# Attention scores with a full-row low part of the key, and RWKV output sums collected by kind of product

## The chip, the cores and the metric

The kernel runs on one core of one Trainium2 chip. The metric is the device time of one execution in microseconds (us); where several runs are given, it is their median. Engines go by the names of the profile: PE is TensorE (PEld its weight loads), DVE is VectorE, ACT is ScalarE, POOL is GpSimd, SP is SyncE.

## What is computed

One sequence of 512 tokens with 1024 channels passes a first block of two hybrid layers (eight attention heads of 64 channels and four retention heads of 128), a feed-forward layer, a token mixer (pooling, a gated linear attention called hgrn, RWKV-7 and a second gated linear attention called gla), a second feed-forward layer. The two places that the change touches are these, cut from the reference:

```python
# chunked_rel_attention
scores = jnp.where(valid, scores + bias[None, None], NEG_INF)
p = jax.nn.softmax(scores, axis=-1)
out = jnp.einsum("bnhqk,bnkhd->bnqhd", p, vb)

# rwkv7_scan, per head with S in (N_v, N_k)
s_kk = jnp.einsum('bhvk,bhk->bhv', S, kk_t)
S = (S * w_t[:, :, None, :] - s_kk[..., None] * (kk_t * a_t)[:, :, None, :]
     + v_t[..., :, None] * k_t[:, :, None, :])
return S, jnp.einsum('bhvk,bhk->bhv', S, r_t)
```

`scores` is the product of queries and keys of one head. The RWKV output is then normalised over each head's 64 channels.

## The kernel before

All products are of fp32 quality. The large ones split each operand into a high and a low part (type fp32r) and take three matmuls: high·high, low·high and high·low. These are the lines L210 to L212, called `mm`, 128x512 each, which make up most of PE's work. The smaller ones, transposes among them, are fp32 matmuls, for which the trace has two records each.

**First block.** `layer` runs eight units p. For p < 4 a unit projects the queries, keys, values and gate of two attention heads; for p >= 4 of one retention head. The scores, the softmax and the product with the values of unit p - 1 (`core()`) are emitted behind the projections of unit p, so that PE finds projection matmuls (`mm`) to run while the softmax goes on; the scheduler sets the final order of each engine's queue. A tile of 128 rows holds both heads' q and k, 64 channels (rows) each. `stacked` (L415 to L431) splits them for the scores. In `qs` of head h the rows of the head (`own`) hold the high part of q and the other 64 rows its low part; `ks` holds the high part of k in both halves. So one matmul over 128 rows, L456, gives high·high plus low·high. The third product needs the low part of k, `kl`: one tile for both heads, each head in its own 64 rows, made by a DVE subtraction for each head (L429, 64x512). L457 multiplies with it over 64 rows: PE then works as an array of 64 rows and 128 columns, which the trace writes as 64*128, and not as 128*128.

`attention` goes over four blocks t of 128 queries; block t needs 128(t + 1) keys. For both heads it takes the scores into a PSUM bank of the pool `psa` (two banks), adds the bias and takes the maximum on DVE (L463, one instruction with a second one that reads the accumulator), the exponential on ACT (L466), the reciprocal and the scaling on DVE (L467, L468). PE transposes the result (`pt`, L472), ACT copies it (`pT`, L474), and PE multiplies it with the values (`po`, L480, an array of 128*64). In the same stretch DVE scales projection results (L395: `fa` is q, `k`, `g` the gate) and splits weights (L189), and ACT casts weights (L188).

**Retention** (p >= 4) loads a tile `decay` by a DMA on SP's queue (two buffers).

**Mixer.** The four mixers are generators, whose steps are run in an order written out by hand (`MIX_ORDER`). RWKV is worked in two halves c of two heads each, with eight chunks n of 64 tokens. Its last step sums the output `pO` (L1072 to L1087), for each chunk n and head h: RH·S (the state, none for n = 0; L1082, array 128*64), MN·KV (L1084, 64*64) and LQ·X (L1086, 64*64). Chunk n lies in the 64-row half n % 2 of one PSUM bank, and the three matmuls of each (n, h) are one accumulation group. 46 matmuls, 92 records; the whole stands twice in the program, for c = 0 and c = 1. Then DVE takes statistics (L1091 to L1097), ACT normalises (`on`, L1100), DVE scales and adds (L1102, L1104), PE transposes (`pt`, L1107).

Of the kernel before, what the change touches and what calls it, by code (L numbers as in the profile page):

```python
# [8 lines left out]
F32 = mybir.dt.float32  # L9
F32R = mybir.dt.float32r  # L10
# [3 lines left out]
ALU = mybir.AluOpType  # L14
# [3 lines left out]
T = 512  # L18
D = 1024
NT = T // 128  # L20
# [92 lines left out]
class Build:  # L113
# [235 lines left out]
    def layer(self, l):  # L349
        nc = self.nc  # L350
        b1 = self.b1
# [60 lines left out]
                nc.scalar.activation(out=t[:, tt, :], in_=ps, func=AF.Copy, scale=rtm[:, tt:tt + 1])  # L412
            return t

        def stacked(q, k):  # L415


            qs, ks = [], []
            kl = b1.tile([128, T], F32R, tag="kl", name="kl", bufs=2)
            for h in range(2):  # L420
                own, other = slice(64 * h, 64 * h + 64), slice(64 - 64 * h, 128 - 64 * h)
                t = b1.tile([128, T], F32R, tag="qs", name="qs", bufs=4)
                nc.scalar.copy(t[own], q[own])
                nc.vector.tensor_tensor(out=t[other], in0=q[own], in1=t[own].bitcast(F32), op=ALU.subtract)
                qs.append(t)
                t = b1.tile([128, T], F32R, tag="ks", name="ks", bufs=4)
                nc.scalar.copy(t[own], k[own])
                nc.scalar.copy(t[other], k[own])
                nc.vector.tensor_tensor(out=kl[own], in0=k[own], in1=t[own].bitcast(F32), op=ALU.subtract)  # L429
                ks.append(t)  # L430
            return qs, (ks, kl)  # L431

        def gate(g, u):
            t = scaled(g, u, 0.5, "g", 8)
# [5 lines left out]
        def attention(p, q, k, v, g):  # L440

            po = self.psc.tile([128, T], F32, tag="c", name="po")
            bias = []
            for h in range(2):
                t = b1.tile([128, T], F32, tag="bias", name="bias", bufs=4)
# [3 lines left out]
            for t in range(NT):  # L449
                n = 128 * (t + 1)  # L450
                pss = []
                for h in range(2):
                    hr = slice(64 * h, 64 * h + 64)
                    ps = self.psa.tile([128, T], F32, tag="a", name="s")[:, :n]
                    qt = q[h][:, t * 128:(t + 1) * 128]
                    nc.tensor.matmul(ps, lhsT=qt, rhs=k[0][h][:, :n], start=True, stop=False)  # L456
                    nc.tensor.matmul(ps, lhsT=qt[hr], rhs=k[1][hr, :n], start=False, stop=True)  # L457
                    pss.append(ps)
                pts = []
                for h in range(2):  # L460
# [9 lines left out]
                    for kt in range(t + 1):  # L470
                        ks = slice(kt * 128, (kt + 1) * 128)
# [44 lines left out]
        v = None  # L516
        for p in range(8):
            if p < 4:
                q = scaled(0, p, 0.125, "fa", 2, self.tmp)
                k = scaled(1, p, 1.0, "k", 2)  # L520
                q, k = stacked(q, k)
            else:
                if p == 4:
                    nc.gpsimd.tensor_tensor(out=CR, in0=self.cosT, in1=R, op=ALU.mult)
                    nc.gpsimd.tensor_tensor(out=SR, in0=self.sinT, in1=R, op=ALU.mult)
                q = rotated(4, p - 4, "qs")
                k = rotated(5, p - 4, "ks")
            if p % 2 == 0:
                v = values(vw if p == 0 else vload(2 if p < 4 else 6, (p % 4) // 2))
            g = gate(3 if p < 4 else 7, p % 4)  # L530
            y.append(g)
            if core is not None:
                core()
            if l == 0 and p == 1:
                self.tables()
            core = (lambda f=(attention if p < 4 else retention), a=(p % 4, q, k, v, g): f(*a))
# [300 lines left out]
    def rwkv(self, e, c):  # L837
# [9 lines left out]
        def psa(shape, name):  # L847
            return self.psa.tile([128, *shape], F32, tag="a", name=name)
# [219 lines left out]
        for tp in range(2):  # L1068
            nc.vector.tensor_tensor(out=bv[:, 4 * tp:4 * tp + 4, :].rearrange("p (i h) k -> p i h k", h=2),
                                    in0=KV[tp][:, :, 128:256].rearrange("p i (h k) -> p i h k", h=2),  # L1070
                                    in1=sb[:, 8 + 4 * tp:12 + 4 * tp].rearrange("p (i h) -> p i h", h=2).unsqueeze(3).to_broadcast([128, 2, 2, 64]), op=mult)
        po = psa((8, 64), "pO")  # L1072
        for tt in range(NT):
            tp, i = tt // 2, tt % 2
            for cc in range(2):
                r = slice(64 * cc, 64 * cc + 64)
                n = 2 * tt + cc
                for h in range(2):
                    v = 2 * i + h
                    pv = po[r, 2 * tt + h, :]  # L1080
                    if n:
                        nc.tensor.matmul(pv, lhsT=RH[:, h, 64 * n:64 * n + 64], rhs=S[:, n, :],  # L1082
                                         start=True, stop=False)
                    nc.tensor.matmul(pv, lhsT=MN[tp][r, v, 64:128],  # L1084
                                     rhs=KV[tp][r, i, 128 + 64 * h:192 + 64 * h], start=(n == 0), stop=False)
                    nc.tensor.matmul(pv, lhsT=LQ[r, 2 * tt + h, 64:128], rhs=X[tp][r, v, 64:128],  # L1086
                                     start=False, stop=True)  # L1087
        st = self.sm.tile([128, 8, 6], F32, tag="bst", name="bst", bufs=2)
        mv = self.sm.tile([128, 8, 2], F32, tag="bmv", name="bmv", bufs=2)
        for j in range(8):  # L1090
# [395 lines left out]
```

## Time and profile before

| | us |
|---|---|
| median of 3 runs (1694.39 to 1697.08) | 1695.64 |
| the profiled execution | 1697.89 |
| its span in the trace | 1696.1 |
| PE busy | 1669.0 (98%) |
| DVE busy | 986.6 (58%) |
| ACT busy | 628.9 (37%) |

The profiled execution stands 2.25 us above the median, within 1 us of the slowest of the three runs. Its mean granted TensorE clock is 0.988 of full speed. A row of the timeline gives an instruction's start and its recorded duration; PE's matmuls are pipelined, so what one of them costs the queue is the distance from its start to the next start, not the recorded duration.

### The profile page before, as it was taken

To read this page: it belongs to the slowest core of one execution; us is meant where nothing else is said; L and a number is where in the kernel's file an instruction comes from. 1 tells how busy PE (TensorE), PEld (TensorE's weight loads), DVE (VectorE), ACT (ScalarE), POOL (GpSimd) and SP (SyncE) were. 2 spreads that over 40 slices of the span, in tenths; PEclk is the share of its full clock that TensorE was granted. 3 is DMA by queue.
4 is the path that set the end of the run, shared out by engine and by line. 5 is a ranking of instruction groups with operands and counts; after the bars stand their busy time and mean duration, and the time that the engine had idled before them with its cause. 6 is when DMAs were issued, how large, how long until landed. Compare 5 with 4: busy or idle time off the path is not lost.

```text
span 1696.1 us, 24094 instructions
## 1 busy us (share of the span) xinstructions
PE 1669.0 (98%) x9648; PEld 1337.3 (79%) x9648; DVE 986.6 (58%) x1972; ACT 628.9 (37%) x1077; POOL 62.8 (4%) x59
## 2 busy tenths in 40 slices
PE   8999999999999999999999999999989999999998
PEld 6777787777778788888888877777767888888886
DVE  7684756554475765555533477658858655554322
ACT  6553423454342433222322235327434423332222
POOL 0001110000111000000000100000200000000000
PEclk9999999999999999999999999989979999999999
DMA  8221213422121223333333432212112433333331
GB/s 242 83 84 41 82 56 99 138 75 75 50 81 56 75 86 101 99 100 94 90 113 111 128 87 66 55 38 54 30 38 86 127 97 91 99 99 94 96 98 62
DMA packets 270673, 147.33 MB, mean 87 GB/s; under 512 B 10576, under 2 KB 264288, under 8 KB 270560
## 3 DMA queue, kind: packets, MB, share of 16 engines
q1 hardware_dynamic: 265600, 140.40, 28.6%
q0 software_dynamic: 1280, 4.20, 0.8%
q10 hardware_dynamic: 3680, 1.19, 0.3%
q8 instruction: 76, 1.25, 0.3%
q14 instruction: 37, 0.30, 0.1%
HBM read 141.30 MB, written 4.46 MB: 86 GB/s over the span
## 4 chain that ended last, share of the span: by engine, by line
PE 90%; DVE 6%; ACT 2%; DMA 1%; issue 1%; SPq 0%; DVEq 0%; ACTq 0%; POOLq 0%
PE mm L211 25%; PE mm L212 25%; PE mm L210 25%; PE po L480 2%; PE pt L472 1%; PE s L457 1%; PE po L498 1%; PE s L493 1%; PE s L456 1%; DMA wraw<-in_w_in 1%; DVE wlo L189 1%; PE pO L1084 1%; PE pO L1082 1%; DVE xr L1187 0%; PE bc L286 0%
## 5 line engine op out<-in xcount | busy, mean ns | idle before, releaser
L188 ACT CAST whi<-wraw 128x1024 fp32r<-128x1024 f32 (+2 forms) x244 | 245.1, 1005 | 691.5 <-PE mm L211 479.9
L189 DVE TENSOR_TENSOR wlo<-wraw,whi 128x1024 fp32r<-128x1024 f32 (+2 forms) x244 | 286.9, 1178 | 150.2 <-ACT whi L188 149.5
L593 DVE SCALAR_TENSOR_TENSOR fa<-mm,R 128x512 f32<-128x512 f32 x44 | 30.3, 691 | 107.8 <-PE mm L212 107.8
L589 DVE SCALAR_TENSOR_TENSOR fa<-mm,R 128x512 f32<-128x512 f32 x44 | 30.3, 690 | 90.5 <-PE mm L212 89.2
L210 PE MATMUL mm<-z0h,whi 128*128 128x512 f32 x163 | 67.7, 416 | 5.7 <-ACT z0h L203 5.7
L211 PE MATMUL mm<-z0l,whi 128*128 128x512 f32 x163 | 65.7, 403 | 0.0
L211 PE MATMUL mm<-z7l,whi 128*128 128x512 f32 x163 | 64.8, 398 | 0.9 <-DVE z7l L204 0.9
L212 PE MATMUL mm<-z0h,wlo 128*128 128x512 f32 x163 | 65.6, 402 | 0.0
L210 PE MATMUL mm<-z4h,whi 128*128 128x512 f32 x163 | 65.4, 401 | 0.0
L210 PE MATMUL mm<-z5h,whi 128*128 128x512 f32 x163 | 65.3, 401 | 0.0
L210 PE MATMUL mm<-z7h,whi 128*128 128x512 f32 x163 | 64.5, 395 | 0.7 <-ACT z7h L203 0.7
L212 PE MATMUL mm<-z3h,wlo 128*128 128x512 f32 x163 | 65.1, 399 | 0.0
L210 PE MATMUL mm<-z6h,whi 128*128 128x512 f32 x163 | 65.1, 399 | 0.0
L212 PE MATMUL mm<-z4h,wlo 128*128 128x512 f32 x163 | 65.0, 399 | 0.0
L211 PE MATMUL mm<-z4l,whi 128*128 128x512 f32 x163 | 65.0, 399 | 0.0
L211 PE MATMUL mm<-z3l,whi 128*128 128x512 f32 x163 | 65.0, 399 | 0.0
L212 PE MATMUL mm<-z6h,wlo 128*128 128x512 f32 x163 | 64.9, 398 | 0.0
L211 PE MATMUL mm<-z5l,whi 128*128 128x512 f32 x163 | 64.6, 396 | 0.0
L211 PE MATMUL mm<-z6l,whi 128*128 128x512 f32 x163 | 64.6, 396 | 0.0
L212 PE MATMUL mm<-z1h,wlo 128*128 128x512 f32 x163 | 64.5, 396 | 0.0
L211 PE MATMUL mm<-z2l,whi 128*128 128x512 f32 x163 | 64.5, 396 | 0.1
L210 PE MATMUL mm<-z2h,whi 128*128 128x512 f32 x163 | 64.5, 395 | 0.0
(738 smaller groups left out, 4230.6 us busy)
## 6 DMA issues: line engine op xcount, KB each, us to landing
wraw<-in_w_in SPq DMA_DIRECT2D x90, 512.0 KB, 4.1
wraw<-in_ffn_w_in SPq DMA_DIRECT2D x88, 512.0 KB, 3.8
wraw<-in_ffn_w_out SPq DMA_DIRECT2D x32, 512.0 KB, 3.9
wraw<-in_w_out SPq DMA_DIRECT2D x16, 512.0 KB, 4.3
wraw<-in_ffn_w_out SPq DMA_DIRECT2D x16, 384.0 KB, 3.6
bias<-in_relb SPq DMA_DIRECT2D x16, 256.0 KB, 2.9
x<-in_xT SPq DMA_DIRECT2D x8, 256.0 KB, 5.3
decay<-in_decay SPq DMA_DIRECT2D x8, 256.0 KB, 3.1
```

The lines of the kernel that those rows point to most:

```text
L188: nc.scalar.copy(hi[:, ks, :], raw[:, ks, :])
L189: nc.vector.tensor_tensor(out=lo[:, ks, :], in0=raw[:, ks, :], in1=hi[:, ks, :].bitcast(F32), op=ALU.subtract)
L210: mm(out, lhsT=lh, rhs=rh, start=start, stop=False)
L211: mm(out, lhsT=lh, rhs=rl, start=False, stop=False)
L212: mm(out, lhsT=ll, rhs=rh, start=False, stop=stop)
L456: nc.tensor.matmul(ps, lhsT=qt, rhs=k[0][h][:, :n], start=True, stop=False)
L457: nc.tensor.matmul(ps, lhsT=qt[hr], rhs=k[1][hr, :n], start=False, stop=True)
L472: nc.tensor.transpose(pt[:, ks], s[:, ks], self.ident)
L480: nc.tensor.matmul(po[64 * h:64 * h + 64, t * 128:(t + 1) * 128], lhsT=v[:, kt, vc:vc + 64], rhs=pts[h][:, ks], start=(kt == 0), stop=(kt ...
L493: nc.tensor.matmul(ps, lhsT=k[:, kt * 128:(kt + 1) * 128], rhs=q[:, T - n:], start=True, stop=True)
L589: nc.vector.scalar_tensor_tensor(out=a2, in0=pg, scalar=0.5, in1=R, op0=ALU.mult, op1=ALU.mult)
L593: nc.vector.scalar_tensor_tensor(out=a2, in0=pu, scalar=0.5, in1=R, op0=ALU.mult, op1=ALU.mult)
```

## The change

Two parts, which have nothing to do with each other.

**Scores.** `stacked` makes one `kl` tile for each head and writes the low part of k into both halves, by two subtractions instead of one: 16 subtractions of 64x512 before, 32 after. The tiles of unit p take the buffers of `decay` for even p and those of `kl` for odd p. The second score matmul (L458 after, L457 before) then uses all 128 rows, as the first does, and so also adds low·low.

**RWKV output.** The 46 matmuls are the same, but go in three parts: all of RH·S, then all of MN·KV, then all of LQ·X, each with n falling from 7 to 0. One accumulation group for each 64-row half of the bank takes the place of one for each (n, h).

```diff
--- before.py
+++ after.py
@@ -412,11 +412,10 @@
                 nc.scalar.activation(out=t[:, tt, :], in_=ps, func=AF.Copy, scale=rtm[:, tt:tt + 1])
             return t
 
-        def stacked(q, k):
-
-
-            qs, ks = [], []
-            kl = b1.tile([128, T], F32R, tag="kl", name="kl", bufs=2)
+        def stacked(q, k, spare):
+
+
+            qs, ks, kls = [], [], []
             for h in range(2):
                 own, other = slice(64 * h, 64 * h + 64), slice(64 - 64 * h, 128 - 64 * h)
                 t = b1.tile([128, T], F32R, tag="qs", name="qs", bufs=4)
@@ -426,9 +425,12 @@
                 t = b1.tile([128, T], F32R, tag="ks", name="ks", bufs=4)
                 nc.scalar.copy(t[own], k[own])
                 nc.scalar.copy(t[other], k[own])
-                nc.vector.tensor_tensor(out=kl[own], in0=k[own], in1=t[own].bitcast(F32), op=ALU.subtract)
                 ks.append(t)
-            return qs, (ks, kl)
+                kl = b1.tile([128, T], F32R, tag=spare, name="kl", bufs=2)
+                for half in (own, other):
+                    nc.vector.tensor_tensor(out=kl[half], in0=k[own], in1=t[own].bitcast(F32), op=ALU.subtract)
+                kls.append(kl)
+            return qs, (ks, kls)
 
         def gate(g, u):
             t = scaled(g, u, 0.5, "g", 8)
@@ -450,11 +452,10 @@
                 n = 128 * (t + 1)
                 pss = []
                 for h in range(2):
-                    hr = slice(64 * h, 64 * h + 64)
                     ps = self.psa.tile([128, T], F32, tag="a", name="s")[:, :n]
                     qt = q[h][:, t * 128:(t + 1) * 128]
                     nc.tensor.matmul(ps, lhsT=qt, rhs=k[0][h][:, :n], start=True, stop=False)
-                    nc.tensor.matmul(ps, lhsT=qt[hr], rhs=k[1][hr, :n], start=False, stop=True)
+                    nc.tensor.matmul(ps, lhsT=qt, rhs=k[1][h][:, :n], start=False, stop=True)
                     pss.append(ps)
                 pts = []
                 for h in range(2):
@@ -518,7 +519,7 @@
             if p < 4:
                 q = scaled(0, p, 0.125, "fa", 2, self.tmp)
                 k = scaled(1, p, 1.0, "k", 2)
-                q, k = stacked(q, k)
+                q, k = stacked(q, k, ("decay", "kl")[p % 2])
             else:
                 if p == 4:
                     nc.gpsimd.tensor_tensor(out=CR, in0=self.cosT, in1=R, op=ALU.mult)
@@ -1069,22 +1070,28 @@
             nc.vector.tensor_tensor(out=bv[:, 4 * tp:4 * tp + 4, :].rearrange("p (i h) k -> p i h k", h=2),
                                     in0=KV[tp][:, :, 128:256].rearrange("p i (h k) -> p i h k", h=2),
                                     in1=sb[:, 8 + 4 * tp:12 + 4 * tp].rearrange("p (i h) -> p i h", h=2).unsqueeze(3).to_broadcast([128, 2, 2, 64]), op=mult)
+
+
         po = psa((8, 64), "pO")
-        for tt in range(NT):
-            tp, i = tt // 2, tt % 2
-            for cc in range(2):
+        seen = [False, False]
+        for part in range(3):
+            for n in reversed(range(8)):
+                tt, cc = n // 2, n % 2
+                tp, i = tt // 2, tt % 2
                 r = slice(64 * cc, 64 * cc + 64)
-                n = 2 * tt + cc
                 for h in range(2):
                     v = 2 * i + h
-                    pv = po[r, 2 * tt + h, :]
-                    if n:
-                        nc.tensor.matmul(pv, lhsT=RH[:, h, 64 * n:64 * n + 64], rhs=S[:, n, :],
-                                         start=True, stop=False)
-                    nc.tensor.matmul(pv, lhsT=MN[tp][r, v, 64:128],
-                                     rhs=KV[tp][r, i, 128 + 64 * h:192 + 64 * h], start=(n == 0), stop=False)
-                    nc.tensor.matmul(pv, lhsT=LQ[r, 2 * tt + h, 64:128], rhs=X[tp][r, v, 64:128],
-                                     start=False, stop=True)
+                    if part == 0:
+                        if n == 0:
+                            continue
+                        lhs, rhs = RH[:, h, 64 * n:64 * n + 64], S[:, n, :]
+                    elif part == 1:
+                        lhs, rhs = MN[tp][r, v, 64:128], KV[tp][r, i, 128 + 64 * h:192 + 64 * h]
+                    else:
+                        lhs, rhs = LQ[r, 2 * tt + h, 64:128], X[tp][r, v, 64:128]
+                    nc.tensor.matmul(po[r, 2 * tt + h, :], lhsT=lhs, rhs=rhs, start=not seen[cc],
+                                     stop=part == 2 and n < 2 and h == 1)
+                    seen[cc] = True
         st = self.sm.tile([128, 8, 6], F32, tag="bst", name="bst", bufs=2)
         mv = self.sm.tile([128, 8, 2], F32, tag="bmv", name="bmv", bufs=2)
         for j in range(8):
```

PE's queue at the first scores of a head pair in layer 1, between the projections `mm`. Before:

```order
L212 MATMUL mm<-z7h,wlo 128x512
L456 MATMUL s<-ks,qs 128x128
L457 MATMUL s<-kl,qs 128x128
L456 MATMUL s<-ks,qs 128x128
L457 MATMUL s<-kl,qs 128x128
L210 MATMUL mm<-z0h,whi 128x512
L456 MATMUL s<-ks,qs 128x256
L457 MATMUL s<-kl,qs 128x256
L211 MATMUL mm<-z0l,whi 128x512
L456 MATMUL s<-ks,qs 128x256
```

After:

```order
L212 MATMUL mm<-z7h,wlo 128x512
L457 MATMUL s<-ks,qs 128x128
L458 MATMUL s<-kl,qs 128x128
L457 MATMUL s<-ks,qs 128x128
L458 MATMUL s<-kl,qs 128x128
L210 MATMUL mm<-z0h,whi 128x512
L457 MATMUL s<-ks,qs 128x256
L458 MATMUL s<-kl,qs 128x256
L211 MATMUL mm<-z0l,whi 128x512
L457 MATMUL s<-ks,qs 128x256
```

The rows stand in the same order; it is the array of the `kl` rows that changes, from 64*128 to 128*128, which this listing doesn't print. Over the attention of both layers PE's queue changes its array 239 times before and 126 times after. Of the 64 `kl` matmuls before, 50 have a full-array matmul on both sides, 14 come behind a `po`.

PE's queue at the first RWKV output sum. `pS` is the last step of the state S. Before, the start of it (the piece of three rows goes on to n = 7):

```order
L212 MATMUL mm<-z3h,wlo 128x512
L1084 MATMUL pO<-KV,MN 64x64
L1086 MATMUL pO<-X,LQ 64x64
L1084 MATMUL pO<-KV,MN 64x64
L1086 MATMUL pO<-X,LQ 64x64
L1082 MATMUL pO<-S,RH 64x64
L1084 MATMUL pO<-KV,MN 64x64
L1086 MATMUL pO<-X,LQ 64x64
L1082 MATMUL pO<-S,RH 64x64
```

After, all of it:

```order
L212 MATMUL mm<-z3h,wlo 128x512
L1092 MATMUL pO<-S,RH 64x64 x14
L1092 MATMUL pO<-KV,MN 64x64 x16
L1092 MATMUL pO<-X,LQ 64x64 x16
L210 MATMUL mm<-z4h,whi 128x512
L211 MATMUL mm<-z4l,whi 128x512
```

(The listing prints the output's shape, 64x64, for all three.) What was a change of kind at each row is now three runs, and what stands ahead and behind is the same.

DVE's queue at the first `stacked` of layer 0. Before:

```order
L395 SCALAR_TENSOR_TENSOR g<-mm,R 128x512
L424 TENSOR_TENSOR qs<-fa,qs 64x512
L429 TENSOR_TENSOR kl<-k,ks 64x512
L424 TENSOR_TENSOR qs<-fa,qs 64x512
L429 TENSOR_TENSOR kl<-k,ks 64x512
L395 SCALAR_TENSOR_TENSOR fa<-mm,R 128x512
L437 SCALAR_TENSOR_TENSOR g<-th,g 128x512
```

After:

```order
L395 SCALAR_TENSOR_TENSOR g<-mm,R 128x512
L423 TENSOR_TENSOR qs<-fa,qs 64x512
L431 TENSOR_TENSOR kl<-k,ks 64x512 x2
L423 TENSOR_TENSOR qs<-fa,qs 64x512
L431 TENSOR_TENSOR kl<-k,ks 64x512 x2
L439 SCALAR_TENSOR_TENSOR g<-th,g 128x512
```

Each `kl` row is now two instructions.

## Rows read from the trace of the kernel before

**Rows 1.** The page, part 1 (busy us, share, instructions) and part 4 (chain).
```profile
PE 1669.0 (98%) x9648; PEld 1337.3 (79%) x9648; DVE 986.6 (58%) x1972; ACT 628.9 (37%) x1077; POOL 62.8 (4%) x59
...
PE 90%; DVE 6%; ACT 2%; DMA 1%; issue 1%; SPq 0%; DVEq 0%; ACTq 0%; POOLq 0%
```

**Rows 2.** Timeline of PE, layer 1, first head pair: start, recorded us, instruction.
```profile
355.60 0.39 PE L212 MATMUL mm<-z7h,wlo 128*128 128x512 f32 x1
355.82 0.22 PE L456 MATMUL s<-ks,qs 128*128 128x128 f32 x1
...
356.74 0.50 PE L210 MATMUL mm<-z0h,whi 128*128 128x512 f32 x1
357.07 0.28 PE L456 MATMUL s<-ks,qs 128*128 128x256 f32 x1
357.29 0.38 PE L457 MATMUL s<-kl,qs 64*128 64x256 f32 x1
357.60 0.50 PE L211 MATMUL mm<-z0l,whi 128*128 128x512 f32 x1
357.94 0.28 PE L456 MATMUL s<-ks,qs 128*128 128x256 f32 x1
```

**Rows 3.** Timeline of DVE, the same stretch.
```profile
356.02 0.69 DVE L395 SCALAR_TENSOR_TENSOR g<-mm,R 128x512 f32<-128x512 f32 x1 [1.66 <-PE mm L212]
356.63 0.28 DVE L463 CUSTOM_DVE_ANT_0 s<-s,bias 128x128 f32<-128x128 f32 x1
356.84 0.08 DVE L463 DVE_READ_ACCUMULATOR2_ANT mx<- 128x1 f32 x1
```

**Rows 4.** Line L429 by itself: duration ns min/median/max, first and last start.
```profile
L429 DVE TENSOR_TENSOR kl<-k,ks x16: 676/686/691, 38.0 to 423.7; 64x512 fp32r<-64x512 f32 x16
```

**Rows 5.** Windows, layer 0: start:end, length, busy us of each engine, granted clock, DMA.
```profile
70.00:108.00 38.00, 37.82 (x223) 30.17 (x223) 35.56 (x81) 16.75 (x32) 3.69 (x2) 1.00 0.15 42
```

**Rows 6.** Timeline of PE in the first RWKV output sum: two periods of it.
```profile
1109.23 0.33 PE L1082 MATMUL pO<-S,RH 128*64 128x64 f32 x2
...
1109.86 0.33 PE L1082 MATMUL pO<-S,RH 128*64 128x64 f32 x2
```

**Rows 7.** Windows around both RWKV output sums.
```profile
1107.37:1113.07 5.70, 5.70 (x58) 4.55 (x58) 0.00 (x0) 0.00 (x0) 0.00 (x0) 1.00 0.24 70
1113.07:1119.11 6.04, 6.04 (x37) 4.62 (x37) 0.00 (x0) 0.00 (x0) 0.00 (x0) 0.50 0.00 0
1119.11:1123.92 4.81, 4.81 (x13) 3.81 (x13) 3.12 (x24) 0.04 (x1) 0.00 (x0) 0.56 0.00 0
1238.34:1250.86 12.52, 12.52 (x93) 9.77 (x92) 1.49 (x3) 0.00 (x0) 0.00 (x0) 0.68 0.08 22
1250.86:1258.34 7.48, 7.48 (x29) 5.13 (x32) 4.21 (x28) 0.81 (x2) 0.00 (x0) 0.63 0.00 0
1263.20:1267.00 3.80, 3.80 (x13) 2.95 (x14) 3.80 (x7) 1.69 (x4) 1.00 (x2) 0.55 0.43 111
```

**Rows 8.** Timeline of PE: two products that alternate between two tiles.
```profile
1076.02 1.15 PE L973 MATMUL pP<-zt,Lo 64*64 64x64 f32 x32
1077.10 0.49 PE L1227 MATMUL po<-gS,qb 128*128 128x128 f32 x2
...
1267.41 0.57 PE L1158 MATMUL pkv<-hvt,kbt 128*64 128x64 f32 x12
1267.91 0.50 PE L210 MATMUL mm<-ysh,whi 128*128 128x512 f32 x1
```

**Rows 9.** Timeline of PE in pG, as it passes from one tile to the other.
```profile
1091.21 0.22 PE L1038 MATMUL pG<-KV 64*64 64x64 f32 x1
1091.22 0.27 PE L1036 MATMUL pG<-Bt,X 64*64 64x64 f32 x1
```

**Rows 10.** Timeline after the second sum: DVE, and PE's wait.
```profile
1258.34 0.69 DVE L737 SCALAR_TENSOR_TENSOR hg<-mm,Rm 128x512 f32<-128x512 f32 x1 [2.44 <-PE mm L212]
...
1263.19 1.19 PE L210 MATMUL mm<-ysh,whi 128*128 128x512 f32 x2 [4.30 <-ACT ysh L200]
```

## The prediction

> **What bounds the kernel now.** I read the page first: PE is busy 98% of the span, and the chain that ended last runs 90% over PE [rows 1]. So time is won where PE's queue itself gets shorter, and it is kept only as far as no other engine then makes PE wait. Next come PE's timelines at the two places of the change, where distances from start to start are to be read, not recorded durations. Then DVE's timeline beside the first place, to see who releases what PE needs next, and a table of windows around the second, for the granted clock.
>
> In the attention, a projection matmul of 512 columns in the full array takes 0.22 us to the next start (355.60 to 355.82). Around an L457, which uses 64 rows, it goes slower: 357.07, 357.29, 357.60, 357.94, that is 0.87 us for a 256-column L456, a 256-column L457 and a 512-column L211 [rows 2]. All three start beside a change of array, or end beside one. At the plain pace of 0.22 us for 512 columns, halved for 256, the three would take 0.11 + 0.11 + 0.22 = 0.44 us. An L457 that stands alone thus costs 0.43 us over its work; as the starts are rounded I take 0.40, which is 0.20 us for each of its two changes of array. The work itself is no longer with 128 rows than with 64, as I read it: only the columns stream.
>
> In the RWKV sums one chunk with its two heads, 12 records, takes 1109.23 to 1109.86 twice over, that is 0.63 us for each (n, h) [rows 6], and at 1113.07 the granted clock falls from 1.00 to 0.50, so 2.4 to 1.2 GHz. It stays low in part of the 4.81 us behind the sum (mean 0.56); the second sum and the 7.48 us behind it have 0.68 and 0.63 [rows 7]. What PE did before each fall was this string of 64-row and 64-column matmuls with a change of array at two of three steps.
>
> **Part 1, scores.** *Removed:* 239 changes of array become 126, which is 113 fewer, at 0.20 us 22.6 us gross. They spread evenly over eight head pairs (four a layer).
>
> *Taken back at once.* The third score matmul of a pair needs a PSUM bank which the first one filled and which DVE empties. DVE does that behind L395, which scales the last projection: L395 starts at 356.02, as soon as that projection (the L212 of 355.60) is out, the L463 follows at 356.63, and its second instruction ends at 356.84 + 0.08 = 356.92 [rows 3]. The third score starts at 357.07 [rows 2]. None of this chain gets shorter by the change. PE loses four changes of array (0.8 us) ahead of that third score, but can start it no earlier than 356.92, 0.15 us before; with some time for the release I take 0.10 us. So of four changes for each pair, 32 in all, remains 8 x 0.10 = 0.8 us, and the other 81 give 81 x 0.20 = 16.2 us. Together 17.0 us. Later score tiles wait for the same two banks, with more room; I take nothing for that, and as a bound a second stall of the same size, 8 x 0.7 = 5.6 us.
>
> *Added:* 16 subtractions of 0.686 us on DVE [rows 4], 11.0 us. They stand beside PE's projections, well ahead of the scores that need them (the first pair's `kl` rows are at 38 us [rows 4] and its scores behind all projections of the next unit). DVE has room in layer 1; in layer 0 it doesn't: between 70 and 108 us it is busy 35.56 of 38.00 us [rows 5]. There four of the subtractions, 2.7 us, could show. What covers them is that PE itself has work there for 37.82 of 38.00 us, DVE's lateness being slack in the weight buffers; I take nothing, and 11.0 us as the far bound if all were exposed. The `kl` tiles in the buffers of `decay` let the first loads of `decay` (SP's queue, behind them weight loads) wait until the scores of pair 2 are done, which is over a whole unit ahead of their use: nothing, by the order of the queue.
>
> **Part 2, RWKV output.** *The sums themselves.* Two products in the trace show what such matmuls cost without changes of array, when neighbours lie in different tiles: pP, 32 records of 64*64, 1076.02 to 1077.10, 1.08 us or 0.034 each; pkv, 12 records of 128*64, 0.50 us or 0.042 each, entry and exit included [rows 8]. After the change PE's row has 28 records of RH·S, then 64 records of 64*64: 28 x 0.042 + 64 x 0.034 = 3.3 us. Before they take 5.70 + 6.04 = 11.74 us and 12.52 us [rows 7]. This saves 8.4 and 9.2 us. Unlike in pP, two neighbours now lie in the same tile before the other tile's two come. pG goes in longer blocks per tile, and there the second head's L1036 starts 0.01 us behind the first head's L1038, while that head's own later ones are still to come [rows 9]: the blocks overlap.
>
> *The clock.* In 3.3 us of dense matmuls I expect no fall. Then the stretch behind the first sum takes 4.81 x 0.56 = 2.7 us, 2.1 less. Behind the second, 7.48 x 0.63 = 4.7 us; of these 2.8 us I take 2.5, since DVE's chain of statistics must also be through before `hg` at 1258.34 [rows 10] goes on. What follows there, ACT's normalisation until PE starts again at 1263.19 after 4.30 us idle [rows 10], moves along unchanged. S is complete before each sum begins, so that starting with n = 7 costs no wait.
>
> First sum 8.4 + 2.1 = 10.5, second 9.2 + 2.5 = 11.7, together 22.2 us.
>
> **Sum.** 17.0 + 22.2 = 39.2 us off the profiled execution, 1697.89 - 39.2 = 1658.7 us. That execution stands 2.25 us above the median; against the median, 1695.64 - 39.2 = 1656.4, and I write 1656.5 us. Own range, from single terms off by a fifth: 1651 to 1662.
>
> **The rivals.**
>
> *A second wait in the softmax.* As PE gets to the transposes earlier, it waits for DVE and ACT, and DVE has 11.0 us more to do. Price 5.6 us (the bound above) to 11.0 us: 1662 to 1667.5. For it: the third score shows that the DVE chain doesn't shrink, and layer 0's DVE is full [rows 5]. Against: PE has projections between all later steps. Chance 0.15.
>
> *No overlap in the sums.* Each record costs what it does before less the changes: (0.63 - 0.20) / 6 = 0.072 us, 92 records 6.6 us, so 3.3 us more in each sum: 1663. If the clock then falls as before, 2.1 + 2.5 us more: 1668. Against: rows 8 and 9. Chance 0.15, some of it for partial forms.
>
> A related one has a rule behind it: the matmuls start strictly in the order of the queue. Then the two records of one matmul and the next of the same tile keep their distance, and only the passage to the other tile is free; half way between 3.3 and 6.6 us is 5.0 us, or 3.4 us more in all: 1660, which lies in the forecast's own range. This is what the Trainium skill says ("TensorE: Matmul & The Clock Gate", The mechanism: matmuls keep program order in start and end). Here the trace doesn't agree as to starts, with 0.01 us between L1038 and the later head's L1036 [rows 9].
>
> *No stall at the third score*, because the order of DVE is kinder than I read it: 5.6 us less, 1651. Against: L395 stands ahead of L463 after the change too. Chance 0.08.
>
> *Not the rows.* The long distances around L457 come from something that stays, such as a second matmul into the same bank. Then part 1 gives nothing: 1656.5 + 17.0 = 1673.5. Against: L210 to L212 go into one bank in succession at 0.22 us [rows 2]. With it goes the case that a change is not carried out as written, which the order of the queues speaks against. Chance 0.04.
>
> *Slower than before.* DVE's added subtractions delay the weight split (L189), which sits in the same queue, so that PE runs dry at a head pair and the clock falls. Such an event has a price in the trace: 4.30 us idle [rows 10], and behind it 3.80 us with a mean clock of 0.55, which lose 3.80 x 0.45 = 1.7 us [rows 7]; 6.0 us together. From 39.2 / 6.0 = 6.5 on, so seven of the eight head pairs, the kernel is slower; with all eight, 1656.5 + 48 = 1704.5 us. For it only the full DVE of layer 0 [rows 5]; in layer 1 there is room. Chance 0.03.
>
> **How the numbers follow.** Forecast 0.55, second wait 0.15, no overlap 0.15, no stall 0.08, not the rows 0.04, slower 0.03. The range reaches from below the case without a stall, 1649, to nearly the far ends of the second wait and of no overlap, 1667; outside lie "not the rows", slower, and the tails of the two. A measurement of this kernel tells some 0.2% (3.4 us) from no change. All cases but the last, and a mixture of all bad ones, are over that: faster 0.96, same 0.01, slower 0.03.
>
> **What would show it.** PE's timeline at a head pair: L457 and L458 in succession at 0.11 to 0.12 us for 256 columns, 0.22 for the projection behind; the third score within 0.1 us of the end of L463's second instruction, with PE idle some 0.6 us ahead of it. In the sums: pO from first start to the next mm in 3.0 to 3.5 us, granted clock 1.00 there and in the next 3 us, and DVE's idle time ahead of L1091 down from some 12 to some 3 us. The forecast is wrong if PE shows more idle time ahead of `pt`, or if the clock in the stretch behind a sum is still near 0.6.

## The result, and the profile after

The changed kernel takes 1658.24 us (median of 4 runs, 1657.79 to 1661.66); the kernel before, run beside it, 1696.12 us (1694.39 to 1697.08). The ratio is 0.9782, 95% interval [0.9765, 0.9799]. The forecast was 1656.5 us, with a range from 1649 to 1667. The span of the profiled execution is 1656.4 us, 39.7 us less than before; the medians differ by 37.9 us.

Busy time of the changed kernel, page part 1 (before: [rows 1]):

```profile
PE 1624.5 (98%) x9648; PEld 1315.8 (79%) x9648; DVE 995.4 (60%) x1988; ACT 628.4 (38%) x1077; POOL 62.7 (4%) x59
```

PE's busy time is 44.5 us less, DVE's 8.8 us more (11.0 us of added subtractions), and PE's share is the same 98%: PE is still the bound, with a shorter queue. It is idle for 31.9 us of the span where it was for 27.1: so 4.8 of the 44.5 us come back, in the net, as waits (rows of waits below).

PE's timeline at the scores of the same head pair as [rows 2], start, recorded us, instruction:

```profile
347.20 0.22 PE L457 MATMUL s<-ks,qs 128*128 128x128 f32 x1
347.26 0.28 PE L458 MATMUL s<-kl,qs 128*128 128x128 f32 x1
347.37 0.27 PE L457 MATMUL s<-ks,qs 128*128 128x128 f32 x1
347.49 0.27 PE L458 MATMUL s<-kl,qs 128*128 128x128 f32 x1
347.60 0.45 PE L210 MATMUL mm<-z0h,whi 128*128 128x512 f32 x1
348.35 0.39 PE L457 MATMUL s<-ks,qs 128*128 128x256 f32 x1 [0.31 <-DVE mx L464]
348.58 0.28 PE L458 MATMUL s<-kl,qs 128*128 128x256 f32 x1
348.69 0.39 PE L211 MATMUL mm<-z0l,whi 128*128 128x512 f32 x1
348.93 0.27 PE L457 MATMUL s<-ks,qs 128*128 128x256 f32 x1
```

The low part's matmul (L458) goes at the full array's pace: 348.58 to 348.69, 0.11 us for 256 columns, and the L211 behind it 0.24 us. The three steps that took 0.87 us in [rows 2] take 0.58 us (348.35 to 348.93), and 0.23 us of that is the first of them, which comes out of a wait. That wait stands ahead of 348.35: the projection of 347.60 takes 0.23 us at the usual pace, so that PE could have gone on at 347.83. DVE beside it (before: [rows 3]):

```profile
347.40 0.69 DVE L395 SCALAR_TENSOR_TENSOR g<-mm,R 128x512 f32<-128x512 f32 x1 [1.66 <-PE mm L212]
348.01 0.28 DVE L464 CUSTOM_DVE_ANT_0 s<-s,bias 128x128 f32<-128x128 f32 x1
348.21 0.08 DVE L464 DVE_READ_ACCUMULATOR2_ANT mx<- 128x1 f32 x1
```

L395 starts at 347.40, as soon as the last projection is out, as before; behind it the two parts of L464 end at 348.21 + 0.08 = 348.29. The third score follows 0.06 us later. PE's waits put this in one row, with a wait of RWKV's in the mixer (`pLQ`, 1.0 us once in the kernel before) and the one transpose that is late (us in total, times, longest):

```profile
PE s L457 <- DVE mx L464: 3.0, 8, 0.8
PE pLQ L923 <- DVE MN L930: 2.8, 2, 1.9
...
PE pt L473 <- DVE s L469: 1.0, 1, 1.0
```

The sums, PE's timeline of the first one (before: [rows 6]), and a table of windows over both sums and what lies behind (columns as in [rows 7]: busy us of PE, PEld, DVE, ACT, POOL, granted clock, DMA):

```profile
1089.99 1.15 PE L1092 MATMUL pO<-S,RH 128*64 128x64 f32 x28
1091.07 1.20 PE L1092 MATMUL pO<-KV,MN 64*64 64x64 f32 x32
1092.05 1.15 PE L1092 MATMUL pO<-X,LQ 64*64 64x64 f32 x32
1093.13 0.50 PE L210 MATMUL mm<-z4h,whi 128*128 128x512 f32 x1
```

```profile
1089.99:1093.13 3.14, 3.14 (x94) 3.00 (x93) 0.00 (x0) 0.00 (x0) 0.00 (x0) 1.00 0.44 131
1093.13:1096.04 2.91, 2.91 (x16) 2.37 (x14) 2.61 (x21) 0.05 (x1) 0.00 (x0) 1.00 0.00 0
1210.29:1213.42 3.13, 3.13 (x93) 3.00 (x92) 1.49 (x3) 0.00 (x0) 0.00 (x0) 1.00 0.14 41
1213.42:1218.24 4.82, 4.82 (x31) 3.43 (x32) 4.09 (x28) 0.82 (x2) 0.00 (x0) 1.00 0.11 31
```

Three runs of one kind take 1.08, 0.98 and 1.08 us, 3.14 us in place of 11.74, and the clock is 1.00 in all four windows, where from 1113.07 us on [rows 7] had 0.50 to 0.68. Behind the second sum PE's next step comes after the same idle time as in [rows 10]:

```profile
1223.10 1.22 PE L210 MATMUL mm<-ysh,whi 128*128 128x512 f32 x2 [4.31 <-ACT ysh L200]
```

So the time goes as follows. The table compares the start of the same instruction in both traces:

| stretch | gained, us | forecast, us |
|---|---|---|
| attention of both layers, scores to last `po` | 14.2 | 17.0 |
| start of layer 1 (z7h, z7l) | 1.8 | - |
| near 1014 us of before (clock not falling 3.2, a wait at `pLQ` -1.9) | 1.3 | - |
| first sum, and the 4.81 us behind it | 8.6 + 1.9 | 8.4 + 2.1 |
| second sum, and the 7.48 us behind it | 9.4 + 2.7 | 9.2 + 2.5 |
| the rest (later falls of the clock) | -0.3 | - |
| sum | 39.6 | 39.2 |

### The profile page after: what moved, and what is told of

It is laid out like the page before. It is cut to its first block, busy times and chain, and to the rows that moved or that the text cites. A ratio compares the mean times of both kernels' runs of the same rounds, so it can differ in the third digit from the quotient of the medians.

```text
span 1656.4 us, 24106 instructions
## 1 busy us (share of the span) xinstructions
PE 1624.5 (98%) x9648; PEld 1315.8 (79%) x9648; DVE 995.4 (60%) x1988; ACT 628.4 (38%) x1077; POOL 62.7 (4%) x59
## 3 DMA queue, kind: packets, MB, share of 16 engines
q8 instruction: 76, 1.25, 0.3%
## 4 chain that ended last, share of the span: by engine, by line
PE 88%; DVE 7%; ACT 3%; issue 1%; DMA 0%; DVEq 0%; SPq 0%; ACTq 0%
PE mm L211 25%; PE mm L212 25%; PE mm L210 25%; PE po L481 2%; PE po L499 1%; PE pt L473 1%; PE s L494 1%; DVE wlo L189 1%; PE s L458 1%; PE s L457 1%; DVE xr L1194 0%; PE po L1238 0%; PE pO L1092 0%; PE bc L286 0%; DVE g L395 0%
## 5 line engine op out<-in xcount | busy, mean ns | idle before, releaser
L211 PE MATMUL mm<-z0l,whi 128*128 128x512 f32 x163 | 64.8, 397 | 0.0
L211 PE MATMUL mm<-z7l,whi 128*128 128x512 f32 x163 | 64.6, 397 | 0.0
L211 PE MATMUL mm<-z4l,whi 128*128 128x512 f32 x163 | 64.3, 395 | 0.0
L211 PE MATMUL mm<-z2l,whi 128*128 128x512 f32 x163 | 64.2, 394 | 0.1
L210 PE MATMUL mm<-z1h,whi 128*128 128x512 f32 x163 | 64.3, 394 | 0.0
L211 PE MATMUL mm<-z3l,whi 128*128 128x512 f32 x163 | 64.2, 394 | 0.0
L211 PE MATMUL mm<-z6l,whi 128*128 128x512 f32 x163 | 64.2, 394 | 0.0
L211 PE MATMUL mm<-z1l,whi 128*128 128x512 f32 x163 | 64.1, 393 | 0.0
L211 PE MATMUL mm<-z5l,whi 128*128 128x512 f32 x163 | 64.1, 393 | 0.0
```

Source lines behind the costliest of these rows:

```text
L210: mm(out, lhsT=lh, rhs=rh, start=start, stop=False)
L211: mm(out, lhsT=lh, rhs=rl, start=False, stop=False)
```

## The experiments

**Each part alone.** Two kernels: the kernel before with only the hunks on `stacked` and L457, and the kernel before with only the new order of the sums.

> The kernel before with part 1 alone (low part of the key on all 128 rows); the RWKV sums are as before. My theory: the two parts add up. The attention takes some 14 us less by array changes, and the first block up to 16 us if the 1.8 us at the start of layer 1 (z7h and z7l late) go as well; the clock still falls in both sums, 11.7 and 12.5 us each. Median 1680 to 1682 us. Rival (the parts lean on each other, or the gain of the attention comes from the clock or from the sums): a time outside 1677 to 1685 us.

> The kernel before with part 2 alone (sums by kind of product); the scores are as before. My theory: pO takes 3.1 us each instead of 11.7 and 12.5, the stretches behind run at full clock, together 22 to 23 us less: 1673 to 1675 us. Whether the wait of 1.8 us for z7h and z7l at the start of layer 1 is there again shows whether part 1 took it away (then it is here in full) or a late DMA of that one execution (then it is gone or of another size). Rival (sums gain only because PE arrives at them at another time): a time above 1678 us.

Part 1 alone: 1681.03 us against 1695.76, ratio 0.9913 [0.9891, 0.9935]. Part 2 alone: 1674.91 us, ratio 0.9872 [0.9853, 0.9891]. So 14.7 and 20.9 us, 35.6 together, where both at once gave 37.9 in another set of runs; the difference is within the intervals, and both medians lie in the ranges expected. In the trace of part 1 alone everything up to the first sum is 16.0 us earlier (17.4 in the changed kernel, 1.3 of them from near 1014 us), and the sums are as before; in that of part 2 alone nothing but 0.5 us has moved up to 1000 us, and the sums are those of the changed kernel. Windows over the two sums, part 1 alone, then part 2 alone:

```profile
1091.34:1103.37 12.03, 12.03 (x94) 9.40 (x93) 0.00 (x0) 0.00 (x0) 0.00 (x0) 0.72 0.12 36
1222.08:1234.77 12.69, 12.69 (x93) 9.88 (x92) 1.50 (x3) 0.00 (x0) 0.00 (x0) 0.66 0.07 22
```

```profile
1105.73:1108.87 3.14, 3.14 (x94) 3.00 (x93) 0.00 (x0) 0.00 (x0) 0.00 (x0) 1.00 0.45 133
1225.91:1229.05 3.14, 3.14 (x94) 3.00 (x93) 1.49 (x3) 0.00 (x0) 0.00 (x0) 1.00 0.12 35
```

12.0 and 12.7 us with clocks of 0.72 and 0.66, against twice 3.14 us at 1.00. The parts do not lean on each other. Part 2 alone also has a wait at the start of layer 1, of another size, 1.2 us in all against 1.6 in the kernel before:

```profile
312.85 0.51 PE L210 MATMUL mm<-z7h,whi 128*128 128x512 f32 x1 [0.35 <-ACT z7h L203]
314.23 0.50 PE L211 MATMUL mm<-z7l,whi 128*128 128x512 f32 x1 [0.88 <-DVE z7l L204]
```

**Is DVE's added work free?** The changed kernel with all its key subtractions done twice:

```diff
-                for half in (own, other):
+                for half in (own, other, own, other):
```

> The changed kernel with each low part of the key written twice, 64 subtractions of 64x512 instead of 32, so another 22 us of DVE in the two attention stages. My theory: DVE's added work is covered by PE's projections, at most 1 to 2 us in layer 0 where DVE is full: 1658 to 1660.5 us, nothing in layer 1. Rival (DVE is already the bound, and part of the forecast gain was lost to the first 11 us): 5 us or more on top, 1663 to 1680 us.

1659.83 us (1658.51 to 1660.93), ratio 0.9784 [0.9766, 0.9803]: in the range expected, and no interval here tells it from the changed kernel. The trace tells more: layer 0, where DVE is full, loses nothing (at 302 us of before it is 6.9 us ahead, the changed kernel 6.8), while layer 1, where I saw room, loses 1.5 us, at two pairs. DVE at one of them, the changed kernel first, then with the work doubled, and PE in the latter:

```profile
410.64 2.78 DVE L431 TENSOR_TENSOR kl<-k,ks 64x512 fp32r<-64x512 f32 x4
414.08 0.69 DVE L395 SCALAR_TENSOR_TENSOR g<-mm,R 128x512 f32<-128x512 f32 x1 [0.66 <-PE mm L212]
```

```profile
411.28 5.70 DVE L431 TENSOR_TENSOR kl<-k,ks 64x512 fp32r<-64x512 f32 x8
417.01 0.69 DVE L395 SCALAR_TENSOR_TENSOR g<-mm,R 128x512 f32<-128x512 f32 x1
417.62 0.28 DVE L464 CUSTOM_DVE_ANT_0 s<-s,bias 128x128 f32<-128x128 f32 x1
```

```profile
417.97 0.39 PE L457 MATMUL s<-ks,qs 128*128 128x256 f32 x1 [1.24 <-DVE mx L464]
```

Once, the subtractions run through from 410.64 in 2.78 us and leave 0.66 us of idle time ahead of L395. Twice, they take 5.70 us, L395 starts when they are done, at 417.01, and with it the chain of the third score, for which PE waits 1.24 us. So the subtractions are free as long as they end ahead of the last projection; at this pair that holds with 0.66 us to spare, so that another subtraction of 0.69 us would, by this sum, have just used it up.

**The wait at the third score.** The changed kernel with both heads' scores in one bank, for t = 0 and 1 (first kernel) and for t = 0 alone (second). Edit of the first:

```diff
-                    ps = self.psa.tile([128, T], F32, tag="a", name="s")[:, :n]
+                    if t > 1 or h == 0:
+                        bank = self.psa.tile([128, T], F32, tag="a", name="s")
+                    ps = bank[:, :n] if t > 1 else bank[:, h * n:h * n + n]
```

The second has `t > 0` for `t > 1`, both times. With them ran the changed kernel once more.

> The changed kernel with the scores of both heads in one PSUM bank for t = 0 and for t = 1, so that the third and fourth score need not wait for DVE to empty the first two. My theory: the wait of 0.5 us at each of eight third scores goes, 4 us less, unless the fifth score, which now waits for the bank of t = 0, or the transposes take its place: 1654 to 1656 us. Rival (the DVE chain behind L395 sets the pace anyway, and the wait only moves to the next score or transpose): 1657.5 to 1659 us.

> The changed kernel with one PSUM bank for both heads' scores at t = 0 alone. Against e4_bank, the later score tiles keep a bank each and so shouldn't be held up at t = 3. My theory (the wait at the third score is a wait for a bank): it goes, the fourth waits for both of DVE's reads of t = 0, some 0.3 us sooner than in the changed kernel, and this lead is kept: 8 x 0.3 to 0.5 = 2.5 to 4 us less than the changed kernel run beside it. Rival (DVE's softmax chain is the pace from here on): within 1 us of the changed kernel.

> The changed kernel once more, to stand beside the next two on the same chip: 1657 to 1660 us. In its trace, the waits and the falls of the clock that were there by chance in one execution (at the start of layer 1 near 305 us, and near 997 us) may differ; the third scores again start 0.06 us behind DVE's release.

The first: 1655.93 us (1655.32 to 1659.71), ratio 0.9766 [0.9746, 0.9787]. The second: 1656.88 us (1655.03 to 1657.83), 0.9773 [0.976, 0.9787], beside the changed kernel at 1660.32 us (1658.68 to 1661.29), 0.9793 [0.9779, 0.9807]: 3.4 us or 0.2%, with intervals that overlap. All three lie within 0.5 us of the ranges expected. The traces are clearer: both are 2.3 us ahead of the changed kernel by the end of the attention. PE's `s` rows of the first, then two of the second, same head pair as above:

```profile
347.11 0.27 PE L459 MATMUL s<-ks,qs 128*128 128x128 f32 x1
...
347.33 0.33 PE L459 MATMUL s<-ks,qs 128*128 128x256 f32 x1
...
350.34 0.44 PE L459 MATMUL s<-ks,qs 128*128 128x384 f32 x1 [0.25 <-DVE mx L466]
```

```profile
347.05 0.33 PE L459 MATMUL s<-ks,qs 128*128 128x256 f32 x1
...
350.06 0.39 PE L459 MATMUL s<-ks,qs 128*128 128x256 f32 x1 [0.27 <-DVE mx L466]
```

With one bank for each t the third score follows the second at 0.22 us, as the theory says: it was a wait for a bank. But now the fifth waits (350.34), and with t = 0 alone the fourth (350.06), for the same DVE line. In all PE waits as long for DVE at the scores as in the changed kernel, 2.9 us against 3.0:

```profile
PE s L459 <- DVE mx L466: 2.9, 8, 1.3
```

The scheduler also puts the scores at other places among the projections, the seventh 6.48 us behind the first (5.76 in the changed kernel). Of eight times 0.5 us some half is kept: the rival was half right.

**What makes the sum short.** Two kernels change the order inside the sums only. In the first n goes 7, 5, 3, 1, 6, 4, 2, 0, so that the few changes of array stay but neighbours lie in the same half; the second takes two chunks of one head at a time through the three kinds, so that the halves alternate and the array changes 15 times.

```diff
-            for n in reversed(range(8)):
+            for n in (7, 5, 3, 1, 6, 4, 2, 0):
```

```diff
-        for part in range(3):
-            for n in reversed(range(8)):
+        for tt in range(NT):
+            for h in range(2):
+                for part in range(3):
+                    for cc in range(2):
...
-                    nc.tensor.matmul(po[r, 2 * tt + h, :], lhsT=lhs, rhs=rhs, start=not seen[cc],
-                                     stop=part == 2 and n < 2 and h == 1)
+                        nc.tensor.matmul(po[r, 2 * tt + h, :], lhsT=lhs, rhs=rhs,
+                                         start=part == (1 if n == 0 else 0), stop=part == 2)
```

> The changed kernel with the three parts of each RWKV sum in the order n = 7, 5, 3, 1, 6, 4, 2, 0: the same matmuls and the same few changes of array, but neighbours lie in the same 64-row half for half a part. If overlap of the two halves carries the short sum, a sum takes 92 records at 0.058 us, which is the distance of records in one tile in the kernel before (and in the traced sum before its neighbour starts), plus two changes: 5.4 to 5.7 us instead of 3.13, and the kernel is 4.5 to 5.5 us slower, 1662.5 to 1664 us; the clock stays up if sparse tiles are not the cause of its fall. Rival (the changes of array were all of it): 3.1 to 3.4 us and no change of time.

> The changed kernel with each RWKV sum worked off two chunks of one head at a time, RH.S twice, MN.KV twice, LQ.X twice: the two halves of the bank alternate as in the changed kernel, each (n, h) is its own accumulation group as before, and the array changes twice for two chunks, 15 changes instead of 1. With 0.10 to 0.15 us for a change of these small arrays beyond the overlapped pace: 3.1 + 14 x 0.1 to 0.15 = 4.5 to 5.2 us a sum, 1661 to 1663 us. Rival (overlap was all of it): 3.1 to 3.5 us; rival (one accumulation group for each half is needed for the pace): 8 us or more.

1665.37 us (2 runs) and 1666.02 us (2 runs), both above the ranges expected, against 1658.24, or 1660.32 for the changed kernel on the same chip. Windows over the first sum, first kernel, then second:

```profile
1094.47:1099.40 4.93, 4.93 (x94) 4.79 (x93) 0.00 (x0) 0.00 (x0) 0.00 (x0) 1.00 0.27 80
```

```profile
1091.95:1097.08 5.13, 5.13 (x93) 4.05 (x92) 0.00 (x0) 0.00 (x0) 0.00 (x0) 1.00 0.29 84
```

Without the alternation a sum takes 4.93 us, 1.8 more, and less than the 5.4 forecast, since at each passage from one half to the other a few matmuls still overlap; with it, but 14 more changes of array, 5.13 us, 2.0 more, which is 0.14 us for a change. No rival holds: both overlap and the changes count. At the full clock all of the sum before would have taken 15 x 0.63 = 9.4 us [rows 6], 2.3 us less than it did; so of the first sum's 8.6 us 2.3 are the clock, which stays at 1.00 in both experiments, and 1.8 are overlap. The other 4.5 us fall to 27 changes of array (28 inside the sum before, two for each RH·S, and one after), 0.17 us each; at the 0.14 of the second kernel they are 3.8 us, and 0.7 us stay open. Of the 8.2 and 5.7 us by which the two profiled executions are longer, 3.6 and 4.0 us are the sums; another 3.1 and 1.3 us arose near 1000 us, by the clock (below).

**The other changes of array.** 126 are left in the attention, around `po`. The changed kernel with values padded with zeros to 128 columns, so that `po` uses the full array and both heads add into the same rows; then the same with each of the two steps on the bank.

```diff
-                        vc = 128 * (p % 2) + 64 * h
-                        nc.tensor.matmul(po[64 * h:64 * h + 64, t * 128:(t + 1) * 128], lhsT=v[:, kt, vc:vc + 64],
-                                         rhs=pts[h][:, ks], start=(kt == 0), stop=(kt == t))
+                        nc.tensor.matmul(po[:, t * 128:(t + 1) * 128], lhsT=v[2 * (p % 2) + h][:, kt, :],
+                                         rhs=pts[h][:, ks], start=(kt == 0 and h == 0), stop=(kt == t and h == 1))
```

> The changed kernel with the last changes of array in the attention taken out too: values padded with zeros to 128 columns for each head (64 more copies on ACT, memsets on POOL), so that po (128*64 before) uses the full array and both heads add into the same rows. My theory (each change costs 0.1 to 0.2 us by what stands beside it): 126 changes go, but po no longer has two heads side by side, 20 matmuls of 0.218 us = 4.36 us a pair against 4.21 with its exits now; the entries of mm, s and pt come 0.06 to 0.11 us cheaper, 8 x 0.1 = 0.8 less: some 0.65 us a pair, 5 us less in all, 1652 to 1655 us. Rival (the overlap of the two heads is worth more than the changes): 1660 us or more.

> Both steps together, e4_bank and e7_full_po. If they add: 2.3 us and what e7 gives, 1650 to 1653 us. If PE is by now ahead of DVE's softmax chain, the second gain turns into waits of PE for DVE: the time of the better of the two alone, 1653 to 1656 us.

> The step of e10_bank_first on top of e7_full_po (po in the full array). If both gains hold: 4 to 6 us less than the changed kernel run beside it. If the waits for DVE and ACT eat the second, as in e9_po_bank: 2 to 3 us less.

1656.31 us (1654.27 to 1658.08), ratio 0.976 [0.9744, 0.9777]; with the first bank step 1658.59 us, 0.9775 [0.9761, 0.979]; with the second 1657.71 us, 0.978 [0.9766, 0.9794]. The gain of the first is 1.9 us against the changed kernel's first median, 4.0 us against the second, taken on the same chip, and 3.1 us in the trace by 700 us, less than the forecast of 5. (In its trace the clock also falls to 0.50 at the second pair of layer 0, from 99.0 us on, where the changed kernel's stays at 1.00.) The steps don't add: the first combination lies above both cases expected, the second, 2.6 us below the changed kernel on the same chip, is the case in which waits eat a gain. PE's waits, full array alone, then with the first bank step:

```profile
PE s L463 <- DVE mx L470: 4.4, 9, 1.8
```

```profile
PE s L465 <- DVE mx L472: 3.0, 8, 1.4
PE po L488 <- ACT pT L483: 2.2, 4, 1.0
```

PE now waits 4.4 us for DVE at the scores (3.0 in the changed kernel), and, combined, 2.2 us for ACT's copies ahead of `po`. The softmax chain has caught up with PE; part of what is taken off PE in the attention from here on comes back as a wait. Against the changed kernel's first measurement none of these versions is surely faster; against the second, on the same chip though not run beside it, full `po` alone is, since [0.9744, 0.9777] and [0.9779, 0.9807] don't overlap.

## Why the prediction was right, and where it was off

**Where PE's time was to be won** held: PE is the bound before and after, and both parts shorten its queue.

**The price of a change of array, 0.20 us for 81 of them,** was too high. I took it from an L457 between matmuls of 256 and 512 columns [rows 2], but other neighbours differ. Sums of PE's distances from start to start, first pair of layer 1, third score to last `po`:

| kind of row | before | after |
|---|---|---|
| L456 / L457 (`ks`) | 1.53 | 1.24 |
| L457 / L458 (`kl`) | 2.21 | 1.34 |
| `mm` | 5.91 | 5.61 |
| `pt` | 2.68 | 2.39 |
| `po` | 4.21 | 4.21 |

1.75 us for ten fewer changes (26 became 16), 0.175 each instead of 0.20. With the third score that is 1.86 us a pair against the 2.1 us forecast, in seven of eight pairs. (A transpose, `pt`, has one record in these traces, 160 for 160, and not two.)

What a change does can be seen in the weight loads (PEld), here for the `kl` row and the projection behind it, before, then after:

```profile
357.29 0.18 PEld L457 LDWEIGHTS s<-kl,qs 64*128 64x128 f32 x1
357.60 0.19 PEld L211 LDWEIGHTS mm<-z0l,whi 128*128 128x128 f32 x1
```

```profile
348.46 0.19 PEld L458 LDWEIGHTS s<-kl,qs 128*128 128x128 f32 x1
348.58 0.19 PEld L211 LDWEIGHTS mm<-z0l,whi 128*128 128x128 f32 x1
```

The matmuls of these loads start at 357.29 and 357.60 [rows 2], and at 348.58 and 348.69: at a change of array a load starts together with its matmul, otherwise some 0.12 us ahead, while the matmul before it runs. So it is at all 239 changes in the attention before (0 to 3 ns ahead), and where the array stays the load is ahead by 0.11 to 0.23 us in the median of each kind of row. That the lost head start is the whole price of a change is not shown.

**The wait at the third score** held: L464's second part ends at 348.29, the score starts at 348.35, and it stands 1.15 us behind the first score where it stood 1.25 before [rows 2]: 0.10 us of 0.8 are kept. Two kernels showed that it is a wait for the bank.

**The second wait in the softmax** (rival, 0.15) came true at one pair, the second of layer 0, where DVE is full [rows 5]: 0.8 us at a score and 1.0 us at a transpose (rows of waits above). That pair gained 1.0 us instead of 2.1. It is also where one of my signs of being wrong, more idle time ahead of `pt`, came up: PE's waits before have no such row. The four added subtractions of the pair, 2.7 us, are not shown to be the cause: with twice as many the third score there stands 2.96 us behind the first, in the changed kernel 3.04. 7 x 1.86 + 1.0 + 0.2 us ahead of the first scores make the 14.2 us.

**DVE's subtractions at nothing:** right for the time, as far as doubling them shows. The reason was only half right: what decides is whether they end ahead of the last projection and not how full DVE is (doubled, they cost layer 1 and not layer 0).

**The sums at 3.3 us each:** 3.14 us. Matmuls of two halves overlap although two lie in one tile before the other's two, so the case without overlap falls, and with it the strict order of starts, for which the forecast had 5.0 us a sum. The two experiments give the sizes, 1.8 us and 0.14 us a change. DVE's idle time ahead of its statistics went from 23.2 us over both sums to 5.2, as forecast.

**The clock** stayed up in and behind the sums as forecast, 1.9 and 2.7 us against 2.1 and 2.5.

**What I had not forecast** are 1.8 us at the start of layer 1 and 1.3 us near 1014 us. The first is a weight that ACT casts ahead of z7h in its queue, and for which it waits until a DMA has brought it. ACT's timeline, before and after:

```profile
311.02 1.05 ACT L188 CAST vhi<-wraw 128x1024 fp32r<-128x1024 f32 x1 [2.35 <-DMA wraw<-in_w_in]
```

```profile
302.41 1.05 ACT L188 CAST vhi<-wraw 128x1024 fp32r<-128x1024 f32 x1 [0.52 <-DMA wraw<-in_w_in]
```

The DMA was issued at the same place of the queue, 305.7 us before and 298.9 after, and took some 5.4 and 3.5 us. PE's wait for z7h and z7l is there in the kernel before (1.6 us) and with part 2 alone (1.2); of the eleven traces with part 1 three have 0.4 to 0.9 us of it (full `po`, full `po` with the first bank step, and the sums by two chunks), and eight have none or at most 0.2, part 1 alone among them. So it varies among kernels with the same scores, but is largest in the two without part 1; what decides it, and whether the edit has a share in the 1.8 us, I can't show.

The second is the sum of two things. In the kernel before the clock falls to 0.50 at 1014 us; in the profiled execution of the changed kernel it doesn't, and by 1021 us of before that execution is 3.2 us further ahead. Then PE waits 1.9 us for DVE at `pLQ` (rows of waits above), where before it had no wait, and 1.3 us remain. Window of the profiled execution of the changed kernel, then of the same kernel in a second one:

```profile
990.00:1020.00 30.00, 27.85 (x167) 20.82 (x166) 19.91 (x41) 15.95 (x23) 0.00 (x0) 1.00 0.19 53
```

```profile
990.00:1020.00 30.00, 27.84 (x144) 20.23 (x144) 18.07 (x36) 14.71 (x21) 0.00 (x0) 0.89 0.19 53
```

A clock of 1.00 and of 0.89. At the end of the second one's stretch it is 3.1 us behind the first, and it ends 3.1 us later (spans 1656.4 and 1659.5). The other twelve traces all have this fall, with a mean clock of 0.90 or 0.95 from 990 to 1025 us. Where it comes ahead of `pLQ`, the wait there is at most 0.3 us; where it comes behind it or not at all, 1.9 us. So a fall ahead of that wait cost some 1.3 us, and one behind it 3.1.

The profiled execution of after was thus lucky in its clock (0.997 of full speed in the mean, 0.995 in the other three runs, though its time, 1658.14 us, is close to the median), and that of before, 2.25 us above its median, was an unlucky one. That the 39.6 us between the two come so near to the forecast's 39.2 is luck: 2.8 us too many in the attention stand against 3.1 us that I had not forecast. The medians' 37.9 us, and 34.4 us on the chip of the second execution, are the better measure of the gain, and the forecast's sum is high by 1 to 5 us: by the price of a change of array and the second wait (together the 2.8 us), and by an unlucky execution as its base.

## To carry to other kernels

A matmul that used half the rows saved nothing where it stood alone between full ones: look at the distance to the next start around it, and pay a few copies on another engine to keep the array as it is, as long as they end before anything waits for them. Group small matmuls by the shape of array, let neighbours alternate between tiles, and count what the slow clock behind a sparse string costs too. Ahead of booking such a gain, find the next buffer that PE will ask for and who frees it: there the gain ends, and after the first such place it pays to look for the next.

## What the runs showed of the chip that I had not expected

The clock fell to half, 1.2 GHz, while PE was busy without a gap (busy 5.70 of 5.70 us ahead of it, [rows 7]); what PE did there were small matmuls with a change of array at two of three steps. In a sum with half the changes, and halves that alternate, it stayed at 1.00 for all 5.13 us, and in one with a single change and little alternation for all 4.93. Whether the changes, the overlap or the length of the string decides is not separated here.

A change of array costs 0.2 us beside long fp32r matmuls, 0.175 us on the mean of the attention and 0.14 to 0.17 us among 64-column fp32 matmuls. At a change the weight load starts with its matmul and not ahead of it, in the attention and in the first sum of the kernel before.

Two executions of one kernel differ by 3.1 us from a single fall of the clock in a stretch that neither part of the change touches; where a wait of PE for DVE follows it, some 1.9 us of such a fall are made up there.
